# Two layers of a diffusion backbone on one core: the planner orders four engines by when TensorE needs each instruction

## The chip, the core and the metric

The kernel runs on one core of a Trainium2 chip. A core has five engines that run at the same time, each through its own stream of instructions in its own order: TensorE (PE; its weight loads are listed as PEld) for matmuls, VectorE (DVE) and ScalarE (ACT) for elementwise work and reductions, GpSimd (POOL) for the rest, and SyncE (SP), which here issues nearly all DMAs. An instruction that needs another engine's result waits on a semaphore at its place in the stream, and everything behind it in that stream waits too. Operands lie in SBUF, matmul results in the eight banks of PSUM.

The metric is the time of one execution in microseconds of the device (us). Before the change it is 1436.07 us, the median of 3 runs (1434.85 to 1436.29).

## The reference

The reference computes two layers over 1024 latent tokens of width 1024, with 256 context tokens beside them. Cut to what matters:

```python
for i in range(2):
    mod_x, mod_c = silu(c) @ w_mod[i] + b_mod[i], silu(c_ctx) @ w_mod[i] + b_mod[i]   # shift, scale, gate
    hx = rms_norm(x, norm_g[i]) * (1 + sc_x) + sh_x
    hc = rms_norm(ctx, norm_g[i]) * (1 + sc_c) + sh_c
    if i == 0:   # 16 query heads on 4 key/value heads, per-head norm, rotary positions, full softmax
        yx, yc = gqa_axial_mixer(hx, hc, a_w_in, q_g, k_g, a_w_out, cos, sin)
    else:        # 16 heads, each token sees an 8 x 16 window and the context, with a learned bias
        yx, _ = neighbourhood_mixer(hx, hc, b_w_in, rpb, b_w_out)
    x = x + g_x * yx
    ctx = ctx + g_c * yc          # first layer only
return rms_norm(x, final_norm_g)
# in both mixers: y = (attention_output * silu(z)) @ w_out, z from the input projection
```

## The kernel before

**Precision.** Every large product is made of float16 pieces: a float32 operand is split into a high half and the remainder, and a product is three matmuls (high by high, high by remainder, remainder by high). So beside the matmuls there are many *splits*: ScalarE writes the high half, VectorE or POOL subtracts it to get the remainder. For weights that is `load_w` (lines 571 to 579: high half L577 on ScalarE, remainder L578 on VectorE), through a staging tile with four buffers; for softmax probabilities it is `p_split` (L926 on VectorE, L929 on POOL).

**Stages.** (1) The first layer's modulation: `mod_cols` makes shift and scale for one block of 128 columns after another (matmuls L496, a copy L498, the column product L501, the scales L502 and L504). `ln_pre` takes the norms of the token tiles (a sum of squares on ScalarE, L715; mean, L544; power on POOL, L546; scaling, L717), and `h_kt` transposes a block on TensorE (L724), applies scale and shift on ScalarE (L726) and splits it on VectorE (L729, L730). Keys and values follow (L734). (2) The first layer's attention in eight pairs of heads (`a_proj`, `a_att`): projections (L838), row maxima (L868, L869), scores (L987, L988), the exponential on ScalarE (L972, L974), the splits and the products with the values (L935 to L937). (3) The first output projection (`a_out`, L1080) with gate and residual (L1084, L1085), and the second layer's norm (`ln_tile`, L553 to L568, transposes L560), whose stores L1087 put the middle stream into DRAM. (4) The second layer in eight pairs of heads: `b_load` brings the weights of a pair (L1149, then L577 and L578), `b_qk` and `b_vz` project queries, keys, values and gate (L1167, L1199, L1202), `b_att` makes the scores (L1230, L1231), adds the bias and takes the maximum (L1250, L1257), the exponentials (L1268 to L1271), the split, a DMA transpose (L1274) and the products with the values (L1279, L1281). Queries and keys leave their PSUM bank through L1180 to L1185: ScalarE writes the high half (L1184 for keys), VectorE the remainder (L1185), for one head of the pair and then for the other. (5) The output projection and the final norm (`b_out`, L1370 to L1382).

**What sets the order.** The kernel's text is written by generators that `timeline` interleaves by shares of their work; that gives a *program order*. It isn't the order of issue: after the text is complete, the class `Planner` goes through all instructions, builds their dependencies (`graph`), gives each a planned duration (`cost`), and simulates the five engines (`schedule`). In this simulation each engine takes, whenever it is free, one of the instructions that are ready by then: the one with the lowest *key*. The key was the place in program order (matmuls that share the array's columns with the one before them, the `glued` ones, get -1 so that they follow at once). Buffers count as well: a tile can be opened only when the tile before it in its ring has been released, and a pool only when the pools that it replaces are done. SP's issues are held when the simulated DMA queue is 2000 ns ahead. The margin of 100 ns is added to each dependency between engines. At the end, `apply` fixes the simulated order of every engine as the order of issue: on the chip, each engine runs exactly this order, however long things really take.

Of the kernel before, what the change touches and what calls it, by code (L numbers as in the profile page):

```python
# [41 lines left out]
class Planner:  # L42
# [110 lines left out]
    def graph(self):  # L153
        acc = {}
        self.pred = []
        self.node = []
        self.tiles = {}
        pool_of = {}
        released = []
        after = {}  # L160
        owner = {}
        for x in self.ins:
            if type(x).__name__ == "BassTilePoolBoundary":
                for t in x.bass_pool_tiles or []:
                    owner[t.name] = x.bass_pool_name
        gone = []
        seen_alloc = {}
        for x in self.ins:
            k = type(x).__name__
            if k == "BassTilePoolBoundary":  # L170
                if x.op == "alloc":
                    seen_alloc[x.bass_pool_name] = list(gone)
                else:
                    gone.append(x.bass_pool_name)
                continue
            if k == "InstTileManualSchedule" or x.engine.name not in self.ENG:
                continue
            i = len(self.node)
            e = self.ENG[x.engine.name]
            p = set()  # L180
            rd = [b for b in map(self.box, x.ins) if b]
            wr = [b for b in map(self.box, x.outs) if b]
            for bs, w in ((rd, 0), (wr, 1)):
                for t, p0, p1, f0, f1, dram in bs:
                    if str(getattr(t, "space", "")) == "PSUM":
                        h = acc.setdefault(t.name, {})
                        p.update(j for j in h.values() if j != i)
                        h[e] = i
                    else:
                        h = acc.setdefault(t.name, ([], []))  # L190
                        for side in ((1,) if not w else (0, 1)):
                            keep = []
                            for q in h[side]:
                                j, a0, a1, g0, g1 = q
                                hit = a0 <= p1 and p0 <= a1 and g0 <= f1 and f0 <= g1
                                if hit and j != i:
                                    p.add(j)
                                if w and hit and p0 <= a0 and a1 <= p1 and f0 <= g0 and g1 <= f1:
                                    continue
                                keep.append(q)  # L200
                            if w:
                                h[side][:] = keep
                        h[w].append((i, p0, p1, f0, f1))
                    if not dram:
                        r = self.tiles.setdefault(t.name, [t, i, set(), owner.get(t.name)])
                        r[2].add(i)
                        if r[1] != i:
                            p.add(r[1])
            self.node.append(x)
            self.pred.append(p)  # L210
        self.eng = [self.ENG[x.engine.name] for x in self.node]

        self.glued = set()
        first = last = None
        for i, x in enumerate(self.node):
            if self.eng[i] != "PE":
                continue
            ts = tuple(x.tile_size or (128, 128))
            out = x.outs[0].bass_ap.tensor.name if ts[1] < 128 else None
            if out and out == last:  # L220
                self.glued.add(i)
                self.pred[first].update(j for j in self.pred[i] if j < first)
            else:
                first = i
            last = out
        self.cst = [self.cost(x, None, None) for x in self.node]
        self.lck = [self.lock(x) for x in self.node]

        self.need = collections.defaultdict(list)
        self.left = {}  # L230
        self.users = collections.defaultdict(list)
        self.queue = collections.defaultdict(collections.deque)
        self.free = {}
        self.poolusers = collections.Counter()
        for name, (t, i, us, pool) in self.tiles.items():
            self.need[i].append(name)
            self.left[name] = len(us)
            for u in us:
                self.users[u].append(name)
            self.queue[t.cap_key].append(name)  # L240
            self.free.setdefault(t.cap_key, [0.0] * (t.tag_meta.bufs if t.tag_meta else 1))
            self.poolusers[pool] += 1
        self.before = seen_alloc
        self.gone = set(gone)

    def schedule(self, key=None, margin=0.0, scale=None):
        scale = scale or {}
        N = len(self.node)
        key = key or (lambda i: -1 if i in self.glued else i)
        succ = [[] for _ in range(N)]  # L250
        npred = [0] * N
        for i, ps in enumerate(self.pred):
# [4 lines left out]
        done = [0.0] * N  # L257
        start = [0.0] * N
        left = dict(self.left)
        end = collections.defaultdict(float)  # L260
        free = {k: list(v) for k, v in self.free.items()}
        q = {k: collections.deque(v) for k, v in self.queue.items()}
        poolleft = collections.Counter(self.poolusers)
        poolend = collections.defaultdict(float)
# [9 lines left out]
        def opened(i):  # L274

            r = 0.0
            for name in self.need.get(i, ()):
                tl, _, _, pool = self.tiles[name]
                for g in self.before.get(pool, ()):
                    if poolleft[g]:  # L280
                        stuck[("pool", g)].append(i)
                        return None
                    r = max(r, poolend[g])
                k = tl.cap_key
                if q[k][0] != name:
                    stuck[("tag", k)].append(i)
                    return None
                if not free[k]:
                    stuck[("tag", k)].append(i)
                    return None  # L290
                r = max(r, min(free[k]))
            return r

        def offer(i):
            r = opened(i)
            if r is None:
                return
            e = self.eng[i]
            r = max(rdy[i], r + (self.SEM[e] if r else 0))
            heapq.heappush(soon[e], (r, key(i), i))  # L300
# [4 lines left out]
        order = {e: [] for e in engs}  # L305
        count = 0
        while count < N:
            best = None
            for e in engs:
                while soon[e] and soon[e][0][0] <= t[e]:  # L310
                    r, k, i = heapq.heappop(soon[e])
                    heapq.heappush(now[e], (k, i, r))
                u = max(t[e], dma - self.AHEAD) if e == "SP" else t[e]
# [6 lines left out]
                if best is None or c < best:  # L320
                    best = c
            if best is None:
                raise RuntimeError(f"plan stuck at {count} of {N}: {[(k, len(v)) for k, v in stuck.items() if v]}")
            s, e = best
            t[e] = s
            while soon[e] and soon[e][0][0] <= s:
                r, k, i = heapq.heappop(soon[e])
                heapq.heappush(now[e], (k, i, r))
            k, i, r = heapq.heappop(now[e])

            o = opened(i)
            if o is None:
                continue
# [2 lines left out]
                continue  # L336
            for name in self.need.get(i, ()):
                ck = self.tiles[name][0].cap_key
                free[ck].remove(min(free[ck]))
                q[ck].popleft()  # L340
            occ, lat = self.cst[i]
            occ *= scale.get(e, 1.0)
            x = self.node[i]
            if self.lck[i]:
                o2 = "POOL" if e == "DVE" else "DVE"
                s = max(s, lock_end[o2])
# [27 lines left out]
            for name in self.users[i]:  # L374
                left[name] -= 1
                end[name] = max(end[name], fin)
                if not left[name]:
                    tl, _, _, pool = self.tiles[name]
                    free[tl.cap_key].append(end[name])
                    again.append(("tag", tl.cap_key))  # L380
                    poolleft[pool] -= 1
                    poolend[pool] = max(poolend[pool], end[name])
                    if not poolleft[pool]:
                        again.append(("pool", pool))
# [6 lines left out]
            for j in succ[i]:  # L391
                rdy[j] = max(rdy[j], fin + self.SEM[self.eng[j]] + margin if self.eng[j] != e or e != "PE" else 0.0)
                npred[j] -= 1
                if not npred[j]:
                    offer(j)
        self.order, self.start, self.done = order, start, done
        return max(done)

    def apply(self):
        info = mybir.DependencyInfo(mybir.DependencyClass.NoSync, mybir.DependencyReason.DATA)  # L400
        for e, o in self.order.items():
            for a, b in zip(o, o[1:]):
                self.tc.add_manual_dep(self.node[b], self.node[a].name, info, reason="plan")
# [1053 lines left out]
```

## Time and profile before

| | |
|---|---|
| median of 3 runs | 1436.07 us (1434.85 to 1436.29) |
| profiled execution | 1435.4 us |
| its span | 1433.3 us |
| mean granted TensorE clock | 0.996 |
| busy: PE, DVE, ACT, POOL | 1369.1, 970.2, 933.1, 637.5 us |
| moved by DMA | 153.01 MB |

The span is the time from the first to the last instruction of the profiled execution; its own time is the device's for that run. "Busy" adds up the time in which an engine executes an instruction. A row of a timeline gives start and length in us, engine, line and operation, the tile written and the tiles read, their shapes, and a count where like instructions are merged; in brackets stands how long the engine was idle before it, and which instruction released it. A wait's row names the waiting instruction, then what it waited for, then total time, number and longest.

### The profile page before, as it was taken

The page shows a single profiled execution, that of the slowest core. Times are in us where ns is not written, and L with a number is a line of the kernel's source. Part 1 is how long each engine was busy: PE and PEld are TensorE (multiplying, and loading weights), DVE is VectorE, ACT ScalarE, POOL GpSimd, SP SyncE. Part 2 cuts the span into 40 slices and gives each one's busy share as a digit, 9 for nine tenths or more (in the row PEclk, how much of TensorE's full clock was granted, in tenths as well). Part 3 has the DMA queues.
Part 4 walks back from the last instruction along what each step waited for, and adds up shares of the span by engine and source line. Part 5 has one row for each costly group of instructions (what it writes and reads, how often), then busy time and mean ns, then how long its engine had stood idle before and what let it go on. Part 6 is the DMA issues. An engine that isn't in the chain of part 4 may idle for free.

```text
span 1433.3 us, 35760 instructions
## 1 busy us (share of the span) xinstructions
PE 1369.1 (96%) x13874; PEld 951.0 (66%) x13874; DVE 970.2 (68%) x2341; ACT 933.1 (65%) x2226; POOL 637.5 (44%) x871
## 2 busy tenths in 40 slices
PE   5799999999999999999999899999999999999797
PEld 2357777777777777776555476767677676767443
DVE  4697877777777777688234736686676757686833
ACT  3452778786868786788735626776676767776811
POOL 2321677766767676677852201312222222313432
PEclk9999999999999999999999999999999999999999
DMA  9753114143222213144123405575665757567932
GB/s 282 212 149 100 40 24 115 23 122 79 59 79 59 79 43 80 34 141 120 44 89 103 148 29 111 91 157 111 136 120 108 156 95 156 92 153 142 185 102 103
DMA packets 327410, 153.01 MB, mean 107 GB/s; under 512 B 234020, under 2 KB 306372, under 8 KB 327240
## 3 DMA queue, kind: packets, MB, share of 16 engines
q1 hardware_dynamic: 326664, 150.70, 43.5%
q8 instruction: 108, 1.77, 0.5%
q14 instruction: 62, 0.51, 0.1%
q10 hardware_dynamic: 576, 0.03, 0.0%
HBM read 85.65 MB, written 12.06 MB: 68 GB/s over the span
## 4 chain that ended last, share of the span: by engine, by line
PE 84%; DVE 9%; ACT 2%; DMA 2%; issue 2%; POOL 1%; SPq 0%; DVEq 0%; POOLq 0%; ACTq 0%
PE pa L838 13%; PE pb L1167 13%; PE pvz L1199 10%; PE poa L1080 7%; PE pob L1370 5%; PE st L987 5%; PE st L988 4%; PE pm L868 3%; PE pkv L734 3%; PE pv L936 3%; PE pv L937 3%; PE pv L935 3%; PE pvz L1202 1%; PE bpv L1279 1%; DVE bk L1185 1%
## 5 line engine op out<-in xcount | busy, mean ns | idle before, releaser
L929 POOL TENSOR_TENSOR pl<-pf,ph 128x256 f16<-128x256 f32 x544 | 368.6, 704 | 134.8 <-ACT pf L974 110.5
L972 ACT ACTIVATE ph<-st 128x512 f16<-128x512 f32 x320 | 192.4, 603 | 107.3 <-PE st L988 105.7
L929 POOL TENSOR_TENSOR bph<-bpf,bph 128x256 f16<-128x256 f32 (+1 forms) x128 | 98.0, 783 | 339.4 <-ACT bpf L1270 305.9
L838 PE MATMUL pa<-wa,x 128*128 128x256 f16 x1536 | 233.6, 272 | 1.3 <-DVE q16q L664 1.3
L869 DVE TENSOR_REDUCE mxp<-pm 128x1 f32<-128x512 f32 x256 | 170.6, 684 | 49.9 <-PE pm L868 48.2
L1167 PE MATMUL pb<-hb_hi,wb 128*128 128x512 f16 (+1 forms) x640 | 194.1, 359 | 3.2 <-DVE bk L1185 3.2
L974 ACT ACTIVATE pf<-st 128x512 f32<-128x512 f32 x320 | 192.0, 604 | 1.5 <-POOL pl L929 0.5
L1199 PE MATMUL pvz<-wb,hb_hi 128*128 128x256 f16 x1024 | 172.1, 273 | 4.8 <-DVE bk L1185 3.2
L936 PE MATMUL pv<-v,ph 128*128 128x64 f16 x1280 | 162.4, 194 | 0.0
L935 PE MATMUL pv<-v,ph 128*128 128x65 f16 x1280 | 162.2, 193 | 0.0
L937 PE MATMUL pv<-v,pl 128*128 128x65 f16 x1280 | 161.1, 192 | 0.7 <-DVE pl L926 0.5
L838 PEld LDWEIGHTS <-x 128*128 128x128 f16 x1536 | 136.1, 97 | 31.8 <-DVE q16q L664 1.6
L1167 PEld LDWEIGHTS <-wb 128*128 128x128 f16 x960 | 92.4, 98 | 77.0 <-issue 3.1
L935 PEld LDWEIGHTS <-ph 128*128 128x128 f16 x1280 | 121.3, 97 | 32.3 <-issue 1.2
L1199 PE MATMUL pvz<-wb,hb_lo 128*128 128x256 f16 x512 | 139.5, 273 | 0.0
L936 PEld LDWEIGHTS <-ph 128*128 128x128 f16 x1280 | 120.5, 97 | 27.0 <-issue 0.2
L937 PEld LDWEIGHTS <-pl 128*128 128x128 f16 x1280 | 121.2, 99 | 10.3 <-DVE pl L926 1.0
L988 PE MATMUL st<-q,k 65*128 65x512 f16 x320 | 121.7, 381 | 0.0
L987 PE MATMUL st<-q,k 128*128 128x512 f16 x320 | 121.0, 379 | 0.7 <-ACT pf L974 0.5
L1199 PEld LDWEIGHTS <-hb_hi 128*128 128x128 f16 x1024 | 98.2, 98 | 27.0 <-issue 5.6
L1167 PE MATMUL pb<-hb_lo,wb 128*128 128x512 f16 (+1 forms) x320 | 114.7, 358 | 0.0
L868 PE MATMUL pm<-k,q 128*128 128x512 f16 x256 | 92.8, 379 | 2.1 <-DVE mxp L869 1.2
(244 smaller groups left out, 3263.7 us busy)
## 6 DMA issues: line engine op xcount, KB each, us to landing
wg<-in_w_mod SPq DMA_DIRECT2D x64, 256.0 KB, 3.9
wsb<-in_b_w_in SPq DMA_DIRECT2D x64, 256.0 KB, 3.0
wm<-in_w_mod SPq DMA_DIRECT2D x32, 256.0 KB, 6.1
wsa<-in_a_w_in SPq DMA_DIRECT2D x64, 128.0 KB, 2.4
xstage<-in_x SPq DMA_DIRECT2D x8, 512.0 KB, 6.7
wsoa<-in_a_w_out SPq DMA_DIRECT2D x16, 256.0 KB, 3.1
x<-in_x SPq DMA_DIRECT2D x8, 512.0 KB, 4.7
x_d<-x SPq DMA_DIRECT2D x8, 512.0 KB, 3.1
```

The costliest lines, as they stand in the source:

```text
L838: T.matmul(ps[:, :, i, :], hA(a, kt, t), wt[w][:, kt, :], start=n == 0, stop=n == 3 * KT - 1)
L869: V.tensor_reduce(mxs[i][:, t, ch:ch + 1], pm, axis=AX.X, op=ALU.max)
L929: G.tensor_tensor(lo[:, c], p32[:, c], hi[:, c], op=ALU.subtract)
L935: T.matmul(pv[:, t, :], hi[:, c], v[:, 0:65], start=first and t == 0, stop=False)
L936: T.matmul(pv[:, t, 0:HD], hi[:, c], v[:, 65:129], start=False, stop=False)
L937: T.matmul(pv[:, t, :], lo[:, c], v[:, 0:65], start=False, stop=last and t == n - 1)
L972: S.activation(ph, st, AF.Exp)
L974: S.activation(p32, st, AF.Exp)
L987: T.matmul(so, k1[:, g, kc], q1[:, :, i, :], start=True, stop=False)
L988: T.matmul(so, k2[0:65, g, kc], q2[0:65, :, i, :], start=False, stop=True)
L1167: T.matmul(ps[:, 0:n], wt[a][:, kt, which * P:(which + 1) * P], hb[b][:, kt, c0:c0 + n], start=m == 0, stop=m == 3 * KT - 1)
L1199: T.matmul(ps[:, :, j, :], hb[a][:, kt, t * P:(t + 1) * P], wt[w][:, kt, 256:512], start=m == 0, stop=m == 3 * KT - 1)
```

## The change

Only the planner changes; the instructions of the kernel stay as they are. Five things are new.

First, `schedule` remembers which tile's release made room for which (`free` now holds the releasing tile's name, and `came` lists, for the instruction that opens a tile, the tile whose place it took).

Second, `deadlines` works out a due time for every instruction from the last simulation. A TensorE instruction is due at its simulated start less all idle time that TensorE had before it, so as if TensorE never waited. Any other instruction is due at the earliest due time of what depends on it, less its own duration, the semaphore's delay and a margin of 300 ns. An instruction that uses a tile is also due before the instruction that takes over that tile's place. What nothing on TensorE needs is due at the end.

Third, `refine` runs five rounds. In each, TensorE's key is the simulated start of the round before, and the key of VectorE, ScalarE, POOL and SP is the due time; then everything is simulated anew. Of the six plans (the first and the five) the one with the shortest simulated time is kept.

Fourth, `glued` matmuls keep their key of -1 in these rounds too. Fifth, `graph` pins a register move between its neighbours in its engine's stream.

```diff
@@ graph
+        before, moved = {}, set()
+        for i, x in enumerate(self.node):
+            e = self.eng[i]
+            if type(x).__name__ == "InstRegisterMove" or e in moved:
+                self.pred[i].update([before[e]] if e in before else [])
+            (moved.add if type(x).__name__ == "InstRegisterMove" else moved.discard)(e)
+            before[e] = i
@@ schedule
-        key = key or (lambda i: -1 if i in self.glued else i)
+        rank = key or (lambda i: i)
+        key = lambda i: -1 if i in self.glued else rank(i)
...
-                free[ck].remove(min(free[ck]))
+                slot = min(free[ck], key=lambda f: f[0])
+                free[ck].remove(slot)
+                if slot[1] is not None:
+                    came[i].append(slot[1])
...
-                    free[tl.cap_key].append(end[name])
+                    free[tl.cap_key].append((end[name], name))
...
-        self.order, self.start, self.done = order, start, done
+        self.order, self.start, self.done, self.succ, self.came = order, start, done, succ, came
         return max(done)
+
+    def deadlines(self, margin):
+
+        N, start, done, cst = len(self.node), self.start, self.done, self.cst
+        due = [1e18] * N
+        idle = prev = 0.0
+        for a in self.order["PE"]:
+            idle += max(0.0, start[a] - prev)
+            prev = max(prev, start[a] + (cst[a][0] if tuple(self.node[a].tile_size or (128, 128))[1] == 128
+                                         else cst[a][0] / 4))
+            due[a] = start[a] - idle
+        heirs = collections.defaultdict(list)
+        for i, names in self.came.items():
+            for name in names:
+                for u in self.tiles[name][2]:
+                    heirs[u].append(i)
+        for i in sorted(range(N), key=lambda i: -start[i]):
+            e, d = self.eng[i], done[i] - start[i]
+            for j in self.succ[i]:
+                due[i] = min(due[i], due[j] - (0.0 if self.eng[j] == e == "PE" else d + self.SEM[self.eng[j]] + margin))
+            for j in heirs.get(i, ()):
+                due[i] = min(due[i], due[j] - d - self.SEM[self.eng[j]])
+        end = max(done)
+        return [min(v, end) for v in due]
+
+    def refine(self, rounds, margin, deadline):
+
+        best = (max(self.done), self.order)
+        self.log = [best[0]]
+        for _ in range(rounds):
+            due = self.deadlines(deadline)
+            key = [s if e == "PE" else v for s, e, v in zip(self.start, self.eng, due)]
+            best = min(best, (self.schedule(key.__getitem__, margin=margin), self.order), key=lambda b: b[0])
+            self.log.append(max(self.done))
+        self.order = best[1]
@@ kernel
         plan.schedule(margin=100.0)
+        plan.refine(5, 100.0, 300.0)
         plan.apply()
```

More of the change, by code (lines that the diff above doesn't have):

```diff
@@ L260, in schedule @@
         end = collections.defaultdict(float)
-        free = {k: list(v) for k, v in self.free.items()}
+        free = {k: [(f, None) for f in v] for k, v in self.free.items()}
+        came = collections.defaultdict(list)
         q = {k: collections.deque(v) for k, v in self.queue.items()}
@@ L290, in opened @@
                     return None
-                r = max(r, min(free[k]))
+                r = max(r, min(f for f, _ in free[k]))
             return r
```

## The prediction, made before the result

> **What bounds the kernel now.** I read the page's busy times first, then the busy time of each engine in nine stretches, then TensorE's waits, and last the rows around single waits. The page:
>
> ```profile
> span 1433.3 us, 35760 instructions
> ## 1 busy us (share of the span) xinstructions
> PE 1369.1 (96%) x13874; PEld 951.0 (66%) x13874; DVE 970.2 (68%) x2341; ACT 933.1 (65%) x2226; POOL 637.5 (44%) x871
> ```
>
> TensorE is the bound: 1433.3 - 1369.1 = 64.2 us of the span are left. Whether a busy TensorE is also a full one shows in the chain of waits, whose longest piece is one run of output-projection matmuls:
>
> ```profile
> 1370.51 55.05 PE pob L1370 x255
> ```
>
> 55.05 / 255 = 216 ns for each 512-column matmul, back to back, with nothing between. The change leaves the set of matmuls alone, so only the 64.2 us can move. The Trainium skill, Perfetto Trace Analysis, section Identifying the Most-Contended Engine, says to judge TensorE's room by the busy share of weight loads and not by that of matmuls; by that rule 66% would leave a third of the span, some 480 us as an estimate. The 216 ns run disagrees: there the loads have slack and TensorE has none.
>
> Busy time by stretch (start:end, length, then PE, PEld, DVE, ACT, POOL with instruction counts, granted clock, DMA share, GB/s):
>
> ```profile
> 0.00:11.00 11.00, 0.17 (x1) 0.18 (x2) 6.43 (x9) 3.17 (x5) 6.16 (x12) 1.00 0.85 270
> 11.00:22.00 11.00, 6.10 (x31) 3.15 (x32) 4.51 (x12) 5.37 (x9) 1.65 (x3) 1.00 1.14 331
> 22.00:67.00 45.00, 37.06 (x265) 18.47 (x264) 24.11 (x55) 15.39 (x27) 9.22 (x12) 1.00 0.78 233
> 67.00:150.00 83.00, 77.78 (x555) 51.40 (x553) 73.14 (x178) 39.86 (x89) 18.89 (x22) 1.00 0.45 118
> 150.00:800.00 650.00, 647.37 (x7965) 464.72 (x7964) 448.77 (x936) 469.20 (x953) 442.88 (x621) 1.00 0.27 74
> 800.00:850.00 50.00, 45.33 (x264) 26.83 (x262) 28.95 (x53) 24.75 (x55) 9.60 (x12) 0.97 0.37 117
> 850.00:1300.00 450.00, 437.48 (x3996) 320.25 (x3995) 307.79 (x901) 312.65 (x902) 107.38 (x145) 1.00 0.60 120
> 1300.00:1350.00 50.00, 42.28 (x400) 29.80 (x399) 42.34 (x128) 42.99 (x133) 15.62 (x21) 0.97 0.84 168
> 1350.00:1433.00 83.00, 75.55 (x415) 36.22 (x412) 34.16 (x74) 19.69 (x59) 26.10 (x26) 0.97 0.40 118
> ```
>
> TensorE's idle time, length less busy: 10.8, 4.9, 7.9, 5.2, 2.6, 4.7, 12.5, 7.7 and 7.5 us. The first layer's attention (150 to 800) is full to 0.4%; the second layer's pairs (850 to 1300) idle 2.8%, and the hand-over into the output projection 15%. The first 11 us are the first load and its norm, and the last 7.5 us are the final row tile's norm and store behind the last matmul: no order of issue shortens these by much, and I leave both at nothing (a gain of at most some 1 us).
>
> What ends TensorE's idle time in the second layer (850 to 1300), as engine, tile and line, awaited engine, us in total, times, longest:
>
> ```profile
> PE bsn L1230 <- DVE bmx L1250: 4.3, 8, 0.8
> PE pb L1167 <- DVE bk L1185: 3.2, 7, 0.5
> PE pvz L1199 <- DVE bk L1185: 3.2, 7, 0.7
> ```
>
> and at the hand-over (1300 to 1350):
>
> ```profile
> PE bsn L1230 <- DVE bmx L1250: 3.6, 5, 0.9
> PE pob L1370 <- ACT wob L577: 2.0, 1, 2.0
> ```
>
> The two counts of 7 are one wait for each pair after the first.
>
> **The change part by part.** No instruction is added or removed; the planner runs on the host, and the new pins on register moves touch one instruction of POOL's first microsecond. What moves is the order in the streams of DVE, ACT, POOL and SP. Until now a ready instruction with the lowest place in the program went first; now that with the earliest due time does, counted back from TensorE's planned start. Here is what the old rule does, in VectorE's rows around one of the seven waits (pair 1):
>
> ```profile
> 945.06 0.69 DVE L578 SCALAR_TENSOR_TENSOR wb<-wsb,wb 128x512 f16<-128x512 f32 x1
> 945.78 0.69 DVE L1185 SCALAR_TENSOR_TENSOR bk<-pb,bk 64x512 f16<-64x512 f32 x1
> ...
> 949.81 0.82 DVE L926 TENSOR_TENSOR bph<-bpf,bph 128x640 f16<-128x640 f32 x1
> 950.66 0.43 DVE L1185 SCALAR_TENSOR_TENSOR bk<-pb,bk 64x256 f16<-64x256 f32 x1
> ```
>
> ScalarE had finished the other half of these keys before either:
>
> ```profile
> 944.33 0.59 ACT L1184 ACTIVATE bk<-pb 64x512 f16<-64x512 f32 x1
> ...
> 949.26 0.38 ACT L1184 ACTIVATE bk<-pb 64x256 f16<-64x256 f32 x1 [0.61 <-DVE bk L1185]
> ```
>
> The key remainder (L1185), which frees the PSUM bank that TensorE's next group needs, was ready at 944.33 + 0.59 = 944.92 and ran at 945.78, behind a weight split (L578) of 0.69; the second was ready at 949.64 and ran at 950.66, behind a probability split (L926) of 0.82. TensorE took up its next group only when it was through:
>
> ```profile
> 992.00 0.38 PE L1167 MATMUL pb<-hb_hi,wb 128*128 128x512 f16 x1
> ```
>
> That is the row of the group for which the weight split at 945.06 was made: its weights were not wanted for 992.00 - 945.75 = 46 us. So the cover for a split put behind is 46 us long, with VectorE idle for 450 - 307.8 = 142 us of the stretch; putting it back costs nothing, and if that cover were gone it would cost its 0.69 on TensorE. With the key remainder first both waits go: 3.2 + 3.2 = **6.4 us** (bounds: 0 if the planned readiness of L1184 comes after the splits, 6.4). The wait for the score bank (L1250, 4.3 us) is of the same kind only in part, since that pass itself takes 0.55 and TensorE's order puts the next scores close behind: half, **2.1 us** (0 to 4.3). What is late next is the other half of it.
>
> At the hand-over TensorE waits once for the last output weights (L577), 2.0 us, while ScalarE has passes for later tiles in front: **2.0 us** (0 to 7.7, the whole stretch). At the start, VectorE:
>
> ```profile
> 15.18 0.21 DVE L504 TENSOR_SCALAR scol<-pmc,bsc 128x2 f32<-128x2 f32 x1
> 15.30 0.14 DVE L544 TENSOR_SCALAR ms_ln<-xss 128x1 f32<-128x1 f32 x1
> ```
>
> and the sum that this mean needs, on ScalarE:
>
> ```profile
> 13.25 0.19 ACT L715 ACTIVATION_READ_ACCUMULATOR xj<-xstage 128x1 f32 x1
> ```
>
> It was ready at 13.44 and ran at 15.30, behind two passes that wait for a TensorE column product; two more norms, the power on POOL and three transposes queue behind it. **1.9 us** (0 to 4.9). At the change of layers:
>
> ```profile
> 814.34 1.88 DVE L578 SCALAR_TENSOR_TENSOR wb<-wsb,wb 128x512 f16<-128x512 f32 x3
> 816.14 0.74 DVE L555 TENSOR_SCALAR x<-x,rs_ln 128x1024 f32<-128x1024 f32 x1
> ```
>
> with POOL's power before it:
>
> ```profile
> 814.56 0.86 POOL L546 TENSOR_TENSOR rs_ln<-ms_ln,mhalf 128x1 f32<-128x1 f32 x1 [2.03 <-DVE ms_ln L544]
> ```
>
> The scaling of the last token tile was ready at 815.42 and ran 0.72 us later behind weight splits: **0.7 us** (0 to 4.7).
>
> The modulation loop (22 to 67) I take at **nothing** (0 to 7.9). Its idle time repeats once per block of 128 input columns as
>
> ```profile
> 48.48 0.50 PE L501 MATMUL pmc<-sel,mrow 128*128 128x2 f32 x4
> 50.35 0.66 PE L724 MATMUL pl<-idf,xstage 128*128 128x128 f32 x4 [1.37 <-ACT tf L726]
> ```
>
> TensorE's own order puts the column product (L501) behind matmuls of the block before; the scale, the activation (L726) and the next transposes hang on it in one chain, and that order is kept. 67 to 150 is taken at nothing as well (-2 to 5.2).
>
> DMAs are sorted by due time too: on SP the weight loads and the stores of the middle stream now go behind the transposes that TensorE reads soon. Each load's buffer is still freed by the same conversion, so the 46 us lead covers them; none of TensorE's waits above names a DMA, so I take nothing (bounds 0, and a loss of 2.0, what the one late weight costs today).
>
> Against this stand new waits. Every stream runs in its order, and a due time says what is urgent, not that the chip has it ready: an urgent pass put early whose input comes late holds everything behind it. The stretch with most to lose is 150 to 800, idle 2.6 us. I let that double: **2.6 us** lost (bounds: 0, and the second layer's share, 2.8% of 650 = 18.1, which is 15.5 more than now).
>
> Sum: 6.4 + 2.1 + 2.0 + 1.9 + 0.7 - 2.6 = 10.5 us. The profiled execution took 1435.4 us, 2.1 of it outside the span, and lies 0.7 under the median of 1436.07; so 1424.9 for it, **1425.6 us** as a median.
>
> **The rivals.** *More than it says (0.15).* TensorE's key is its last planned start, but only among what the plan holds ready: where the plan shifts, its order shifts too. Then the loop's 7.9 us and the other 4.0 of the layer change can be filled: 10.5 + 7.9 + 4.0 = 22.4, 1413.7 us. For it: a column product moved ahead of its block's matmuls would start that chain early. Against: the key holds exactly the places that the first plan gave.
>
> *No change (0.14).* Each wait removed uncovers the next one at once, as with L1250 behind L1185; or no round beats the first plan and its order is kept. 1434 to 1438 us. Against it: the leads measured above, 0.7 to 1.9 us each, are large against the 0.4 to 0.7 us that the waits last.
>
> *Slower (0.21): 150 to 800 loses its cover.* Here VectorE is 448.8 / 650 = 69% busy, ScalarE 72%, POOL 68%, and TensorE is kept full by passes that happen to come early. If planned durations are off by more than the slack, exponentials or probability splits end behind other work and the stretch idles like the second layer, 15.5 us more; with half of the gains above (6.5) it is 1436.1 + 15.5 - 6.5 = 1445 us. It decides from 2.6 + 13.1 = 15.7 us of idle in that stretch on. For it: planned and real durations do differ, as in
>
> ```profile
> L578 DVE SCALAR_TENSOR_TENSOR wb<-wsb,wb x64: 674/684/1762, 794.9 to 1209.2; 128x512 f16<-128x512 f32 x64
> ```
>
> (shortest, median, longest): one split took 2.6 times the median. Against it: a third of each of the three engines is free there. The Trainium skill, SBUF — State Buffer, section Who interferes with whom, gives a reason: a VectorE pass with two SBUF inputs and a POOL pass that reads SBUF exclude each other for a whole instruction, and the one issued second waits, so that the order decides who pays. The 1762 agrees with it; a new order draws these meetings anew.
>
> **How the numbers follow.** Forecast 0.50 with its own range 1417 to 1433, more 0.15, no change 0.14, slower 0.21. No change can be told from one within 0.2%, 2.9 us. The forecast and "more" are faster: 0.65. The range: down to 1407, a little under the second case, which leaves out some 0.07 where nearly all of the 45.5 us between 11 and 1350 goes; up to 1444, which leaves out about half of the slower case, 0.11.
>
> **What would show it.** Right: the seven-fold waits on L1185 gone; idle in 850 to 1300 about 4 us; 11 to 22 about 3; the loop's idle as before; 150 to 800 at 3 to 6 us. Wrong: waits of TensorE on exponentials or splits (L974, L926, L929) of together over 10 us between 150 and 800, or L1185 still behind L578 in VectorE's rows.

## The result, and the profile after

The changed kernel takes 1422.6 us (median of 4 runs, 1419.89 to 1424.26), the kernel before 1436.18 us beside it (1434.85 to 1438.66): ratio 0.9902, 95% interval 0.9881 to 0.9922, so 13.6 us less. Its profiled execution took 1422.27 us. In the changed file the kernel's own lines stand 48 further down: L1185 is now L1233, L1184 is L1232, L1250 is L1298, L577 and L578 are L625 and L626, L926 is L974, L555 is L603. In the experiments they stand up to 3 further still.

The page's head:

```profile
span 1420.4 us, 35780 instructions
## 1 busy us (share of the span) xinstructions
PE 1368.9 (96%) x13874; PEld 952.3 (67%) x13874; DVE 972.8 (68%) x2341; ACT 933.1 (66%) x2226; POOL 640.9 (45%) x871
```

TensorE's work is what it was (1369.1 us before); the span is 12.9 us shorter, and 12.7 of them are TensorE's idle time, which fell from 64.2 to 51.5 us. The busy time of each engine in the stretches of the prediction (start:end, length, then PE, PEld, DVE, ACT, POOL, granted clock, DMA share, GB/s; the last is 12.6 us shorter):

```profile
0.00:11.00 11.00, 0.66 (x2) 0.29 (x2) 1.59 (x8) 3.53 (x6) 6.07 (x12) 1.00 0.87 267
11.00:22.00 11.00, 7.13 (x50) 3.82 (x50) 4.82 (x12) 3.24 (x7) 1.65 (x3) 0.88 1.17 314
22.00:67.00 45.00, 39.01 (x258) 19.73 (x258) 26.10 (x61) 20.27 (x37) 9.22 (x12) 0.92 0.83 248
67.00:150.00 83.00, 77.78 (x566) 51.28 (x567) 73.21 (x175) 38.60 (x86) 22.42 (x24) 1.00 0.45 115
150.00:800.00 650.00, 648.86 (x7961) 465.06 (x7958) 451.22 (x939) 471.07 (x954) 440.94 (x620) 1.00 0.28 76
800.00:850.00 50.00, 45.33 (x273) 28.13 (x272) 26.10 (x50) 22.00 (x51) 8.13 (x10) 0.93 0.28 89
850.00:1300.00 450.00, 443.65 (x4078) 327.44 (x4077) 324.57 (x922) 320.71 (x929) 115.28 (x152) 1.00 0.62 123
1300.00:1350.00 50.00, 43.77 (x372) 27.02 (x370) 39.46 (x124) 42.27 (x130) 17.81 (x21) 0.97 0.89 192
...
1350.00:1420.40 70.40, 62.66 (x330) 29.55 (x327) 25.72 (x55) 11.44 (x31) 19.38 (x19) 0.96 0.32 105
```

Length less busy gives TensorE's idle time: 10.3, 3.9, 6.0, 5.2, 1.1, 4.7, 6.4, 6.2 and 7.7 us, where it was 10.8, 4.9, 7.9, 5.2, 2.6, 4.7, 12.5, 7.7 and 7.5. Half of the gain is in the second layer's pairs; the rest comes in pieces of 0.5 to 2 us. By the same events in both traces, the second layer's first projection begins at 805.19 us (809.84 before), its last gate projection at 1302.90 (1314.03), and TensorE's last matmul at 1412.28 (1425.17). So 4.6 us are won up to the second layer, 6.5 in it, and 1.8 behind it.

TensorE's waits in the second layer (805 to 1303), with the columns that the prediction has:

```profile
PE plb L608 <- DVE x L603: 4.7, 2, 4.4
PE bsn L1278 <- DVE bmx L1298: 2.0, 5, 0.6
PE pvz L1247 <- DVE bk L1233: 1.7, 7, 0.2
PE pb L1215 <- DVE bk L1233: 1.3, 3, 0.4
PE pvz L1247 <- DVE bsz L1263: 1.0, 4, 0.2
```

The wait at the change of layers (the first row) is as long as before. The score bank's fell from 4.3 to 2.0, and the key remainder's two from 6.4 to 3.0: shorter, not gone. At the hand-over (1302.9 to 1356) the wait for the last output weights, 2.0 us on ScalarE's half and 0.3 on VectorE's, became 0.5; the score bank's fell from 3.6 to 2.4; and a new wait of 2.1 stands there:

```profile
PE bsn L1278 <- DVE bmx L1298: 2.4, 3, 0.9
PE bsc L1278 <- ACT bpf L1319: 2.1, 1, 2.1
...
PE pob L1418 <- DVE wob L626: 0.5, 1, 0.5
```

Why TensorE still waits for the key remainder shows in the pair of the prediction's rows (it calls it pair 1; it is the third of the eight). The row that carries the wait there, before, is not the one at 992.00 us that the prediction shows, which belongs to the next pair. It is this one, at the end of the remainder that began at 945.78:

```profile
946.52 0.38 PE L1199 MATMUL pvz<-wb,hb_hi 128*128 128x256 f16 x2 [0.73 <-DVE bk L1185]
```

In the changed kernel the same matmul waits 0.23 us. Still the remainder does not go first. VectorE's rows ahead of that matmul, where ScalarE's half had ended at 939.62:

```profile
939.88 0.68 DVE L626 SCALAR_TENSOR_TENSOR wb<-wsb,wb 128x512 f16<-128x512 f32 x1
...
940.94 0.69 DVE L1233 SCALAR_TENSOR_TENSOR bk<-pb,bk 64x512 f16<-64x512 f32 x1
```

Later in the same pair, ScalarE's half of the keys:

```profile
944.24 0.38 ACT L1232 ACTIVATE bk<-pb 64x256 f16<-64x256 f32 x1 [0.25 <-DVE bk L1233]
```

and VectorE's rows behind it:

```profile
944.86 0.82 DVE L974 TENSOR_TENSOR bph<-bpf,bph 128x640 f16<-128x640 f32 x1
945.70 0.43 DVE L1233 SCALAR_TENSOR_TENSOR bk<-pb,bk 64x256 f16<-64x256 f32 x1
```

The remainder was ready at 944.24 + 0.38 = 944.62, and at 944.86 VectorE began a probability split of 0.82 us all the same. The order is fixed ahead by the planner. Either the plan ranked the split higher, or it took the remainder to be ready a moment after the split could start; a rule that sorts only what is ready takes the split in the second case, whatever the rank. Over the 42 remainders of the last seven pairs the mean time from the end of ScalarE's half to the start of the remainder is 0.87 us before and 1.11 in the changed kernel: the remainders run later behind their readiness, and TensorE waits less for them all the same.

### The profile page after: what moved, and what is told of

It is laid out like the page before. It is cut to its first block, busy times and chain, and to the rows that moved or that the text cites. A ratio compares the mean times of both kernels' runs of the same rounds, so it can differ in the third digit from the quotient of the medians.

```text
span 1420.4 us, 35780 instructions
## 1 busy us (share of the span) xinstructions
PE 1368.9 (96%) x13874; PEld 952.3 (67%) x13874; DVE 972.8 (68%) x2341; ACT 933.1 (66%) x2226; POOL 640.9 (45%) x871
## 4 chain that ended last, share of the span: by engine, by line
PE 82%; DVE 9%; ACT 4%; issue 2%; DMA 1%; POOL 1%; DVEq 0%; POOLq 0%; SPq 0%; ACTq 0%
PE pa L886 13%; PE pvz L1247 11%; PE pb L1215 10%; PE poa L1128 7%; PE pob L1418 5%; PE st L1036 5%; PE st L1035 5%; PE pm L916 4%; PE pkv L782 3%; PE pv L984 3%; PE pv L983 3%; PE pv L985 3%; PE pvz L1250 1%; PE bpv L1327 1%; DVE bk L1233 1%
## 5 line engine op out<-in xcount | busy, mean ns | idle before, releaser
L985 PEld LDWEIGHTS <-pl 128*128 128x128 f16 x1280 | 121.5, 99 | 10.2
```

The lines of the kernel that those rows point to most:

```text
L985: T.matmul(pv[:, t, :], lo[:, c], v[:, 0:65], start=False, stop=last and t == n - 1)
```

## The experiments

Four questions: does TensorE's order stay (the prediction takes it that it does), which engine's new order carries the gain, where in the program does it arise, and is rank or readiness what the key remainder lacks.

### TensorE's order held, and TensorE's order alone

The first run chains TensorE's instructions in the order of the first plan and takes the last round's orders for the other four engines, whether or not that round's plan is the shortest:

```diff
@@ refine
-        self.order = best[1]
@@ kernel
         plan.schedule(margin=100.0)
+        for a, b in zip(plan.order["PE"], plan.order["PE"][1:]):
+            plan.pred[b].add(a)
         plan.refine(5, 100.0, 300.0)
```

> TensorE is bound to exactly the order of the first plan; the four other engines go by due time (the fifth round, not the best one). Theory A (the prediction's: the gain is in the order of the four engines, TensorE keeps its order): about the gain of the change, 1420 to 1428 us. Theory B (TensorE's own order has shifted in the change, and the two orders only work together): no gain, 1436 us or more, most likely 1445 or more, because TensorE then stops at fixed places for passes that the due order has put later.

Measured: 1457.71 us, ratio 1.0146 (1.0129 to 1.0163). The second run does the reverse. TensorE gets the changed kernel's order, and the others go by their place in the program:

```diff
@@ kernel
         plan.refine(5, 100.0, 300.0)
+        for a, b in zip(plan.order["PE"], plan.order["PE"][1:]):
+            plan.pred[b].add(a)
+        plan.schedule(margin=100.0)
```

> TensorE is bound to the order that it has in the changed kernel; the four other engines go by place in the program again. Theory A: TensorE's shift is worth little, 1433 to 1438 us. A rival, C (all of the gain is TensorE's new order): 1420 to 1427 us. Theory B: slower than before, 1440 us or more.

Measured: 1466.88 us, ratio 1.0210 (1.0195 to 1.0225). TensorE's longest group of waits, first with its order held, then with its order alone:

```profile
PE bsn L1277 <- DVE bmx L1297: 10.9, 15, 3.4
```

```profile
PE bsn L1278 <- DVE bmx L1298: 31.3, 20, 3.2
```

Either half of the change without the other costs 20 to 29 us instead of winning 14: theory B, in both runs. The planner's own simulation has these losses already: it puts the first plan at 1405.2 us, the changed kernel's at 1393.9, and the plans of these two runs at 1427.0 and 1437.4. So they are properties of the orders, and not a gap between plan and chip. Due times around an order that may not yield are worse than no due times. TensorE "keeps its order" only as a preference among what the plan holds ready: the changed kernel's order is another one, and it fits the others' new orders as these fit it. In the trace this shows most at the start. TensorE's stretch up to the first key/value product, and from there to the last modulation column, before:

```profile
0.00:22.27 22.27, 6.54 (x33) 3.53 (x34) 11.21 (x21) 8.54 (x14) 7.80 (x15) 1.00 1.00 301
22.27:61.90 39.63, 33.39 (x248) 16.64 (x246) 20.37 (x45) 11.41 (x19) 5.97 (x7) 1.00 0.83 254
```

and after:

```profile
0.00:26.61 26.61, 11.03 (x72) 5.66 (x73) 7.93 (x24) 8.06 (x13) 7.72 (x15) 0.86 1.02 287
26.61:57.60 30.99, 28.07 (x198) 13.99 (x195) 16.25 (x40) 11.78 (x20) 2.61 (x6) 0.95 0.91 290
```

72 matmuls instead of 33 stand ahead of the first key/value product: modulation products, column products and transposes of later blocks were drawn forward. The product comes 4.3 us later, and the last column 4.3 us earlier; the loop's idle time falls from 6.2 to 2.9 us. (This needs the due times of SP and POOL as well: with those two by place, in the run on two engines below, the first product stands at 22.20 us behind as few matmuls as before, and the loop idles 6.2 us.)

### One engine by due time, and two

Due times for ScalarE alone, the other three by place:

```diff
-            key = [s if e == "PE" else v for s, e, v in zip(self.start, self.eng, due)]
+            key = [s if e == "PE" else v if e == "ACT" else i
+                   for i, (s, e, v) in enumerate(zip(self.start, self.eng, due))]
```

> Only ScalarE goes by due time; VectorE, POOL and SP by place in the program; TensorE as in the change. Theory A, by the prediction's terms: 2.0 us of 13.1 lie on ScalarE, so about 1434 us. Its rival (ScalarE's order feeds the rest: it releases the banks first): 1424 to 1430 us.

Measured: 1431.18 us beside 1437.48, ratio 0.9960 (0.9945 to 0.9975). The same for VectorE alone (`"DVE"` in place of `"ACT"`):

> Only VectorE goes by due time; ScalarE, POOL and SP by place in the program; TensorE as in the change. Theory A, by the prediction's terms: 11.1 us of 13.1 lie on VectorE, so about 1426 us. The rival (ScalarE carries it): 1433 to 1437 us.

Measured: 1432.96 us, ratio 0.9976 (0.9967 to 0.9986). And for both (`e in ("ACT", "DVE")`), POOL and SP by place:

> ScalarE and VectorE go by due time together, POOL and SP by place in the program. If the two gains are of different waits, they add: 6.3 + 4.5 = 10.8 us, about 1426.5 us, with the start as before the change (the first projection of the first layer near 107 us and not 104). If both free the same waits: 1429 to 1432 us, and POOL and SP carry the rest of the change's 13.6.

Measured: 1423.44 us beside 1436.58, ratio 0.9907 (0.9892 to 0.9921). That is the whole change's gain within the intervals. The single gains, 6.3 and 4.5 us, add to 10.8; together they give 13.1. So the due times of POOL and SP are worth nothing that can be told in the whole time, and ScalarE, which the prediction had left almost out, carries at least as much as VectorE. (By the ratios the gains are 5.7, 3.4 and 13.4 us.) In the profiled executions the gains lie in different places, in us against the kernel before:

| due times for | to the second layer's first projection | second layer | from its last gate projection to the end | sum |
|---|---|---|---|---|
| ScalarE | -1.4 | 8.1 | -2.5 | 4.3 |
| VectorE | 2.0 | 2.2 | -2.0 | 2.1 |
| both | 1.9 | 7.3 | 3.0 | 12.2 |
| all four (the change) | 4.6 | 6.5 | 1.8 | 12.9 |

The second layer's gain is ScalarE's. At the hand-over either engine alone loses, and only both together win: that is where they give more than their sum, and it was not followed further. The due times of POOL and SP win 2.7 us ahead of the second layer and lose 2.0 after it (one profile each). The waits in the second layer, with ScalarE's due times alone:

```profile
PE bsn L1279 <- DVE bmx L1299: 2.2, 8, 0.3
...
PE pb L1216 <- DVE bk L1234: 1.0, 3, 0.3
PE pvz L1248 <- DVE bk L1234: 1.0, 4, 0.2
```

and with VectorE's alone:

```profile
PE bsn L1279 <- DVE bmx L1299: 5.2, 11, 1.1
...
PE pvz L1248 <- DVE bk L1234: 1.0, 4, 0.2
PE pb L1216 <- DVE bk L1234: 0.8, 3, 0.3
```

Either brings the waits on the key remainder from 6.4 us to about 2. Emptying the bank is a chain of two passes, ScalarE's half (L1184) and then VectorE's (L1185), and either end can be sped up. But these waits do not tell the two runs apart: the score bank's do, which fall to 2.2 us with ScalarE's due times and rise from 4.3 to 5.2 with VectorE's.

### Where in the program

Due times only from the second layer's first projection on; ahead of it the key is the place in the program, scaled to the plan's length:

```diff
+            b0 = next(i for i, x in enumerate(self.node) if any(o[0].name.startswith("bk1") for o in map(self.box, x.outs) if o))
+            key = [(s if e == "PE" else v) if i >= b0 else i * max(self.done) / len(due)
+                   for i, (s, e, v) in enumerate(zip(self.start, self.eng, due))]
```

> Due times (and TensorE's key from the last plan) only for instructions from the second layer's first projection on; everything before goes by place in the program. By the stages of the two traces 6.6 + 1.1 + 1.8 us lie behind 805 us less what the start brought, so about 8 us: 1428 to 1430 us. If the second layer's gain needed what comes before it: 1433 us or more.

Measured: 1433.0 us beside 1436.58, ratio 0.9974 (0.9963 to 0.9985): a gain of 3.6 us, less than half of what was expected, and at the edge of the rival (1433 us or more: the second layer's gain needs what comes before it). Its trace has both a gain and a loss. From the second pair's first projection to the last gate projection it takes 874.9 to 1314.2 = 439.3 us, where the kernel before takes 866.0 to 1314.0 = 448.0; but the first pair, which holds the change of layers, takes 811.3 to 874.9 = 63.6 us and before 56.2. There TensorE waits for ScalarE's activation of the tokens:

```profile
PE plb L610 <- ACT tfb L614: 7.5, 3, 4.5
```

and VectorE's rows show three weight splits between the two passes that empty the activation's buffer (L617, L618):

```profile
814.43 0.41 DVE L617 CAST hb_hi<-tfb 128x512 f16<-128x512 f32 x1
814.76 1.88 DVE L628 SCALAR_TENSOR_TENSOR wb<-wsb,wb 128x512 f16<-128x512 f32 x3
816.57 0.68 DVE L618 TENSOR_TENSOR hb_lo<-tfb,hb_hi 128x512 f16<-128x512 f32 x1
```

The two kinds of key meet there, and the splits come ahead. Whether the meeting of the keys is the reason was not tried apart; the trace shows that 8.7 us are won from the second pair on and 7.4 lost in the first; with 1.4 lost ahead of the second layer and 2.6 won behind it, the span is 2.5 us shorter. The counterpart has due times up to that projection, and all behind it strictly later and by place:

```diff
+            b0 = next(i for i, x in enumerate(self.node) if any(o[0].name.startswith("bk1") for o in map(self.box, x.outs) if o))
+            key = [(s if e == "PE" else v) if i < b0 else i + 1e9
+                   for i, (s, e, v) in enumerate(zip(self.start, self.eng, due))]
```

> Due times only for what stands ahead of the second layer's first projection in the program; all from there on by place and behind the former. If the two layers' gains simply add: the 4.6 us by which the changed kernel begins the second layer's first projection earlier, so 1431 to 1433 us, and the second layer's own stretch (first projection to the last pvz product) takes 504 us as before. If the first layer's gain needs the second layer's due times at the seam: 1434 to 1437 us.

Measured: 1430.47 us beside 1436.53, ratio 0.9956 (0.9939 to 0.9973), a little under the range for simple adding. Its second layer takes 504.5 us (804.93 to 1309.39; before 809.84 to 1314.03, 504.2) and has the old waits on the key remainder (3.2 and 3.1 us, seven times each). So the gains of the two layers add, and the rival with its 1434 to 1437 is out: 6.1 us are won without any due time in the second layer (4.6 by the spans of the two profiles), and some 7.5 of the 13.6 need them.

### Rank or readiness

Giving the weight splits the lowest rank of all in the first plan changes no engine's order at all; so a picture in which weight splits outrank the key remainder cannot be the cause. The planned times say what is: the 42 remainders of the last seven pairs wait 15.2 us in the first plan after they are ready, and 1.9 of these stand behind passes that were taken after that moment. The rest is one pass in each case, a weight or probability split or a pass on scores or outputs, that had been taken up to 0.6 us before the remainder was ready in the plan. ScalarE's halves of the same keys wait 27.4 us there, and 19.8 of these stand behind passes of higher rank taken after they were ready. (All this was read from the plans and not timed.) So the plan says: readiness on VectorE, rank on ScalarE. Two edits ask the chip. The first plan with the passes that empty the second layer's projection banks ranked first, and no due times:

```diff
-        plan.refine(5, 100.0, 300.0)
+        names = [next((o[0].name for o in map(plan.box, x.outs) if o), "") for x in plan.node]
+        out = {i for i, n in enumerate(names) if n.startswith(("bk1", "bq1", "bq2", "bv1", "bsz", "bth"))
+               and plan.eng[i] in ("ACT", "DVE")}
+        plan.schedule(key=lambda i: -1 if i in out else i, margin=100.0)
```

> The first plan alone, no due times, but the passes of ScalarE and VectorE that empty the projections' PSUM banks in the second layer go first whenever they are planned ready. Theory F (the prediction's term: these passes stand behind others, 6.4 us, and 1.3 on the gate's): 1428 to 1431 us. Rival G (the plan holds them ready only after the other passes are taken, so being first changes little): 1434 to 1438 us.

Measured: 1428.79 us beside 1436.58, ratio 0.9945 (0.9930 to 0.9960). Theory F's time came. A rank among the ready is worth 7.8 us without any due time, and on ScalarE it shows: the first half of a projection of the keys begins 0.18 us after its last matmul in the mean of the last seven pairs, and 0.96 before the change. The waits on the key remainder went to 3.6 us and the score bank's were gone, while the waits on the gate's bank (bsz) are longer than in the changed kernel (1.0 us):

```profile
PE pvz L1247 <- DVE bsz L1263: 4.3, 7, 0.6
PE pvz L1247 <- DVE bk L1233: 2.7, 6, 0.5
PE pb L1215 <- DVE bk L1233: 0.9, 5, 0.2
```

The other side is readiness: let a free engine stand still for up to 100 ns of planned time for something of higher rank.

```diff
+    LOOK = 100.0
@@ schedule
-            while soon[e] and soon[e][0][0] <= s:
+            while soon[e] and soon[e][0][0] <= s + (self.LOOK if e in ("DVE", "ACT") else 0.0):
                 r, k, i = heapq.heappop(soon[e])
                 heapq.heappush(now[e], (k, i, r))
             k, i, r = heapq.heappop(now[e])
+            if r > s:
+                t[e] = s = r
```

Added to the changed kernel:

> The changed kernel, where in addition VectorE and ScalarE may hold still for up to 100 ns of planned time for an instruction with an earlier due time. If the waits left on the key remainders come from a pass that is taken just before the urgent one is ready: 1418 to 1421 us. If not: 1421 to 1425 us, as the changed kernel.

Measured: 1417.59 us beside 1436.58, ratio 0.9869 (0.9852 to 0.9885): the fastest of all, a little below the range given for the first case. Added to the first plan, with no due times (the call of `refine` left out):

> The first plan alone (priority by place, no due times), except that ACT and DVE, when they come free, may stand still for up to 100 ns of planned time for an instruction that outranks the ready ones. Theory H (a projection bank's emptying loses its turn because it becomes ready a moment after a filler has been taken, and not because the filler outranks it): 1429 to 1432 us, and in the second layer TensorE's waits pb<-bk and pvz<-bk fall from 6.4 us in sum to under 4. Rival P (place decides: the filler has the lower place and goes first with a hold too): 1435 to 1438 us, and those waits stay above 5.5 us.

Measured: 1428.14 us beside 1436.53, ratio 0.9938 (0.9920 to 0.9955): theory H, by the waits (3.1 us) and nearly by the time. And added to the plan with the emptying passes first:

> The run with the second layer's emptying passes put first (no due times, 1428.8 us), and the hold of 100 ns added. Theory H: the hold and the first place work together, since a pass that is first among the ready ones still comes too late by a moment: 1424 to 1427 us, waits on bk below 2 us in sum in the second layer. Rival P (first place was all that was missing): 1428 to 1430 us, waits on bk as without the hold.

Measured: 1428.42 us, ratio 0.9938 (0.9918 to 0.9958). The second layer from its second pair on, with the hold alone:

```profile
PE pvz L1250 <- DVE bk L1236: 2.1, 7, 0.3
PE pb L1218 <- DVE bk L1236: 1.0, 6, 0.2
```

and with the hold and due times:

```profile
PE pvz L1250 <- DVE bk L1236: 1.9, 6, 0.6
```

The hold alone halves the key remainder's waits (6.4 to 3.1) and removes the score bank's (4.3 to nothing), at unchanged ranks. Where a hold acts at unchanged ranks, the urgent pass already outranked the filler and lacked only readiness; VectorE's remainders then start 0.53 us after ScalarE's half in the mean, and 0.87 before. Both runs fit what the first plan says. How much of the 13.6 us each part carries is not separated, since an order is planned as a whole and one edit moves many passes. With the hold and the emptying passes first, theory H's 1424 to 1427 us were missed and rival P's words came true: 1428 to 1430 us, and waits on the key remainder (3.6 us) as without the hold. Why these two do not add, where the hold and due times do, is open. In none of the runs faster than before do the key remainder's waits fall below 1.8 us, and the longest left is 0.6 us in the fastest kernel (0.7 before). That they are the two passes' own time was not tried.

The fastest kernel's stretch from its second pair to the last gate projection is 2.3 us short of full:

```profile
862.70:1297.44 434.74, 432.49 (x3988) 319.72 (x3987) 320.36 (x921) 320.67 (x925) 109.26 (x149) 1.00 0.66 128
```

The same stretch took 448.0 us before and 440.3 in the changed kernel (862.6 to 1302.9). Of these 13.3 us, 3.0 are busy time of the same matmuls (435.48 us before, 433.95 in the changed kernel, 432.49 here): in these three, busy time is shorter where TensorE waits less often. What makes it was not tried; it is a part that the prediction's "only the 64.2 us can move" leaves out.

## Why the prediction was right

The time, 1425.6 us forecast and 1422.6 measured, is right, and so is its place: TensorE's idle time, with the second layer first. By its steps it is half right, and that the sum came so near is in good part luck, since two errors cancel. Of its signs of being right none came as written: TensorE still waits for the key remainder ten times, it idles 6.4 us in 850 to 1300 and not 4, 3.9 in 11 to 22 and not 3, the loop's idle time fell, and 150 to 800 lies below the 3 to 6 us. One of its signs of being wrong did come: L1185 still runs behind L578 in VectorE's rows (939.88 and 940.94 above).

*Key remainder, 6.4 us: mis-sized, and its reason was wrong.* The waits fell by 3.4 us. The step "with the key remainder first both waits go" failed: in the changed kernel the remainders still run behind splits that were taken 0.24 and 0.26 us after they were ready, and in the mean later than before (1.11 us for 0.87). The prediction's own lower bound (planned readiness after the splits) named the cause that the plan's times show and the hold supports. That the ready instruction with the lowest place went first is true of the rule, but not the reason for these rows: the splits were taken because the plan did not yet hold the remainder ready. VectorE was also only half of it; ScalarE's due times alone shorten the same waits as much.

*Score bank, 2.1 us: right* (4.3 to 2.0). That the other half would stay is true of the changed kernel only; with a hold it goes too.

*Hand-over, 2.0 us: right, in part by luck.* The wait for the last output weights fell by 1.8 and the score bank's by 1.2, but a new one of 2.1 us on an exponential (L1319) stands in the stretch. With the end, 1.8 us are won from the last gate projection on.

*Start norms, 1.9 us: came for two norms of three, and is mis-sized.* The norm at 15.30 us now runs at 11.19, as soon as ScalarE has its sum, and the next at 12.69 (16.78 before), both ahead of the column's passes; only the last still queues behind the column's scale:

```profile
11.19 0.15 DVE L592 TENSOR_SCALAR ms_ln<-xss 128x1 f32<-128x1 f32 x1 [2.64 <-ACT xj L763]
...
12.69 0.15 DVE L592 TENSOR_SCALAR ms_ln<-xss 128x1 f32<-128x1 f32 x1
...
16.78 0.21 DVE L552 TENSOR_SCALAR scol<-pmc,bsc 128x2 f32<-128x2 f32 x1
16.90 0.14 DVE L592 TENSOR_SCALAR ms_ln<-xss 128x1 f32<-128x1 f32 x1
```

The idle time of 11 to 22 fell by 1.0 us and not by 1.9. TensorE also has more to do there (50 matmuls for 31), and how the 1.0 us divides was not tried. With SP and POOL by place the norms stand where they stood (15.24 us): this gain needs their due times, and the prediction took SP's at nothing.

*Layer change, 0.7 us: nothing.* POOL's power (809.90 us, 0.86 long) and VectorE's rows after it are those of before, 4.7 us earlier:

```profile
809.68 1.88 DVE L626 SCALAR_TENSOR_TENSOR wb<-wsb,wb 128x512 f16<-128x512 f32 x3
811.49 0.74 DVE L603 TENSOR_SCALAR x<-x,rs_ln 128x1024 f32<-128x1024 f32 x1
```

Ready at 810.76, run at 811.49: 0.73 us late, as before.

*Modulation loop, nothing: wrong.* This step rested on the order of that loop being kept. It is not, and 1.9 us of idle time went in that stretch (3.3 by events). This is the rival "more than it says" in its mechanism, without its size: the other 4 us of the layer change did not move.

*150 to 800, a loss of 2.6 us: wrong in sign.* It gained 1.5. TensorE's idle time there is 1.1 us, and the slower rival needed 15.7; no wait on exponentials or splits of any size appeared.

So up to the second layer the sum had a net loss of 0.7 us (1.9 less 2.6) where 4.6 were won; the second layer with its change of layers had 9.2 where it won 6.5; the rest had 2.0 and won 1.8. *SP at nothing: right in the whole time only.* The run that leaves SP and POOL by place has the whole gain, but the start's norms, the loop's gain and 2.7 us of the 4.6 up to the second layer need their due times; behind it they lose 2.0.

## What to carry to other kernels

When a fixed order comes from a planner that gives a free engine whatever is ready, look in the rows for a long filler that starts just before a short urgent pass: a better rank helps only where the urgent pass is ready in the plan, and a short permitted hold won more here (1422.6 to 1417.6 us, each beside its own 1436). An order of one engine is no constant while the others' move: frozen against orders it was not made with it cost 20 to 29 us, and the planner's own simulation could have said so. Before a wait is booked as gain, follow the chain that ends it back over both engines, and book what an undisturbed chain still takes.

## What the runs showed of the hardware

A wait of TensorE can cost more than its length. At the change of layers the same 384 matmuls kept TensorE busy for 51.49 us before and 52.74 after, though the wait in front was 4.7 us in both. The stretches, before:

```profile
809.84:866.00 56.16, 51.49 (x384) 36.55 (x383) 26.31 (x54) 21.66 (x53) 5.94 (x8) 0.97 0.18 56
...
816.80:820.00 3.20, 2.97 (x11) 2.15 (x12) 3.20 (x8) 2.37 (x6) 0.00 (x0) 0.50 0.94 278
```

and after:

```profile
805.19:862.60 57.41, 52.74 (x384) 36.83 (x383) 26.30 (x54) 21.64 (x53) 5.94 (x8) 0.94 0.18 55
...
811.60:818.00 6.40, 5.62 (x18) 3.11 (x19) 5.32 (x10) 5.50 (x14) 0.00 (x0) 0.50 0.79 227
20.00:29.00 9.00, 7.63 (x42) 3.85 (x35) 3.77 (x9) 1.30 (x2) 0.00 (x0) 0.50 0.99 270
```

The granted clock (the third column from the right) falls to 0.50 near the end of the idle time and stays there for at least 3.2 us in the one and 6.4 in the other, mostly with TensorE at work. 5.62 - 2.97 = 2.65 us more of busy time at half the speed is 1.3 us of work undone; 1.25 were lost. The Trainium skill, TensorE: Matmul & The Clock Gate, Part 1: The HAM clock gate, says that the clock is halved after an idle window of some 3.4 us and restored after a busy one, and that these windows run free of the kernel; the two lengths, near one and two windows, agree. So in these two traces the same wait cost one such stretch at half clock, and two.

The last row shows the clock at half in the changed kernel's start, for some 10.2 us (19.4 to 29.6), near three windows. There the Trainium skill's rule of an idle window does not tell the fall: TensorE had stood still for 2.04 us (16.54 to 18.58) and was at work again when the clock fell. In the fastest kernel it fell at 134.7 us for some 3.4 us with no idle time longer than 0.55 us in the 10 us before it. In both, TensorE was busy for only part of the 3.4 us ahead of the fall (1.4 and 2.0 us); from what share on the clock is kept was not measured. The run with due times up to the second layer had the full clock from 20 to 29 us and reached the first key/value product at 26.41 us instead of 26.61, and the second layer at 804.93 instead of 805.19, so there half the clock cost next to nothing; that loads and norms hold the start, and not TensorE, is the likely reason and was not tried.
